# A hybrid decoder layer: products of two weight units in one block, sigmoids behind the last exponentials

## The chip, the cores and the metric

The kernel runs on one core of a Trainium2 chip. The engines that matter are TensorE (PE in the profile; its weight loads are listed as PEld), VectorE (DVE), ScalarE (ACT), GpSimd (POOL) and SyncE (SP, which issues the DMAs). Each works through its own queue in order and waits on semaphores of the others. The metric is the device time of one execution in microseconds; the span in a profile runs from the first to the last instruction, so it is a little shorter.

## The reference, cut to what matters

One decoder layer over 256 positions of width 1024, in float32:

```python
proj  = x @ w_in[l]                      # [q | k | v | B | C | h | gate_attn | gate_conv]
gates = sigmoid(proj[..., off + 3*c:] + b_gate[l])
q, k  = apply_partial_rope(q, cos, sin), apply_partial_rope(k, cos, sin)   # first 16 of 64 dims
y_att = moba_attention(q, k, v) @ w_attn_out[l]
y_cnv = (gate_b * causal_dwconv(gate_c * h_in, conv_w_mix[l])) @ w_conv_out[l]
mix   = (g_att * y_att + g_cnv * y_cnv) @ w_o[l]
x     = layer_norm(DEEPNORM_ALPHA * x + mix, ln1_g[l], ln1_b[l])
u     = causal_dwconv(x @ w_up[l], conv_w_ffn[l])
f     = (silu(u[..., :D_FF]) * u[..., D_FF:]) @ w_down[l]
x     = layer_norm(DEEPNORM_ALPHA * x + f, ln2_g[l], ln2_b[l])
```

There are 8 heads of 64, D_FF is 2816, and the MoBA block is 256 positions, so with 256 positions the attention is plain causal attention: scores, masked softmax, probabilities times v.

## The kernel before, in words

**High and low parts.** Every float32 operand of a product is split into a high part (a rounded copy, made by ACT) and a low part (the rest, a subtraction on DVE). A product of two operands is then three products: high x high, high x low, low x high.

**Units.** The weights lie in memory as chunks of 128 x 2048 numbers, in the order of use; a chunk holds two units of 128 x 1024 in most stages. SP loads chunks into three buffers `raw`. `split_h` (L188) issues the DMA of the chunk two further on and lets ACT write the unit's high part `wh`; `split_l` (L194) lets DVE write the low part `wl`. There are nine buffers of each. The splits run `LA` = 4 to 6 units ahead of the products.

**A unit of columns.** `unit_cols_wide` (L328) computes 128 output columns of the transposed result for all 256 positions. Its activations lie as high and low side by side, so one *wide* product of the weight's high part with 512 columns (L334) does two of the three products; eight of them, over eight slices of the inner dimension, are followed by eight *narrow* ones of the weight's low part with the 256 high columns (L336). The result stands in two halves of one PSUM bank of 512 columns, which are added when the bank is emptied: ACT copies the right half into SBUF and DVE adds the left half.

**The stages.** First 34 warm-up products of zeros (L236), while the first data arrive. Then q, k and v for all heads, chunk by chunk (L539-574), 24 wide products of each inner slice. Then the mixer stage: 28 units of columns, two each for h, c and b of the first half of the convolution channels, the same for the second half, and 16 gate units `g0` to `g15`. The first of them is called `C0` in the code. Then the `y` stage: output products of convolution and attention, times the gates (`mix`, L679); then `w_o` with the first layer norm; then the feed-forward stage and the second layer norm.

**The order in the mixer stage** is written out by hand. `at(u, part, f, ...)` (L463) puts a piece of work beside unit `u`, and `slot(u, products)` (L468) issues, in this order: the unit's products; the PE pieces and then the ACT pieces beside this unit, each in the order in which `at` was called; the split of the high part for unit `u+5`; the split of the low part for unit `u+4`; the DVE pieces, again in the order of the calls. Since engines work in order, this order decides who stands behind whom. Beside the units run:

- `rope` on q and k at C0 and C0+1 (DVE); their transposes on PE, two groups at C0+2 and two at C0+3, and the splits of these one unit later (`qk_h` on ACT, `qk_l` on DVE);
- for head pairs p = 0 to 3: `scores` at C0+4+3p (PE), `masked` one later (DVE), `exps` two later (ACT, exponential); `normalize` at C0+7+5p (DVE), `probs_T` one later (PE, six transposes), `probs_h` and `probs_l` two and three later, `attend` four later (PE), `attend_h` and `attend_l` five later;
- the convolution (`conv1` to `conv4`) and, for every unit, the sum of the two halves of its bank one unit later (`conv_sum_*`, `gate_sum_*`);
- `gate(j)`, the sigmoid of gate unit j on ACT, one unit after its sum. `exps` and `gate` need different function tables of ACT; a change of table is an instruction of its own, ACT_TABLE_LOAD.

Four PSUM banks `acc` serve the units in turn, four banks `ps` serve transposes, scores and attention. The sums of the gates have three buffers `gs`.

**The feed-forward stage** goes over 22 blocks of 128 gate columns (`g`) and 128 value columns (`v`); block i is computed as unit `g`, unit `v`, and the down projection `d` of block i-3, which is 12 wide products (L877). The first two blocks come from another form of product (`up0`) and are transposed by `up0_T`, which is issued behind the first `g` unit of block 2. Both units of a block share a tile of two banks, of which there are two, and the tile is emptied behind unit `v` (`ffn0_act`, `ffn0_dve`). The `slot` of this stage (L916) is a separate function that also runs the splits ahead.

Of the kernel before, what the change touches and what calls it, by code (L numbers as in the profile page):

```python
# [12 lines left out]
AF = mybir.ActivationFunctionType  # L13
ALU = mybir.AluOpType

P = 128
S = 256
# [120 lines left out]
def layer_kernel(ctx: ExitStack, tc: tile.TileContext, x, wpack, cpack, ln1_g, ln1_b, ln2_g, ln2_b, out):  # L138
    nc = tc.nc
# [10 lines left out]
    def acc_bank(name):  # L150
        return psum.tile([P, 512], F32, tag="acc", name=name)

    def ps_bank(name):
        return ps_pool.tile([P, 512], F32, tag="ps", name=name)

    def scratch(shape, name, bufs=None, tag="scr"):
        return tmp.tile(shape, F32, tag=tag, name=name, bufs=bufs or 6)
# [5 lines left out]
    chunks, plan_units, U = plan()  # L163
    blocks = transfers(chunks, plan_units)
    units = [dict(chunk=c, off=off, shape=(k, n), h=None, l=None) for c, off, k, n, _ in plan_units]
# [22 lines left out]
    def split_h(u):  # L188

        issue_dma(units[u]["chunk"] + RAW_BUFS - 1)  # L190
        alloc(u, "h", "wh")
        nc.scalar.activation(units[u]["h"], raw_of(u), AF.Copy)  # L192

    def split_l(u):  # L194

        alloc(u, "l", "wl")
        nc.vector.tensor_tensor(units[u]["l"], raw_of(u), units[u]["h"].bitcast(F32), op=ALU.subtract)  # L197
# [34 lines left out]
    def warm_up(n):  # L232
        for i in range(n):
            nc.tensor.matmul(warm[:, 0:P], zeros, zeros, start=True, stop=True)

    warm_up(34)  # L236

    mask = cst.tile([P, 384], F32, name="mask")
    nc.gpsimd.memset(mask, 0.0)
# [19 lines left out]
    xT = big.tile([P, KT, 2, S], F32R, tag="xT", name="xT")  # L259
# [5 lines left out]
    def bias_gate(j):  # L265
        return consts[:, 132 + j:133 + j]
# [51 lines left out]
    def unit_cols(u, o, bh, bl, n0=0):  # L318

        un = units[u]  # L320
        nk = un["shape"][0]
        for k in range(nk):
            wh, wl = un["h"][:, k, n0:n0 + P], un["l"][:, k, n0:n0 + P]
            nc.tensor.matmul(o, wh, bh[:, k, :], start=k == 0, stop=False)  # L324
            nc.tensor.matmul(o, wh, bl[:, k, :], start=False, stop=False)  # L325
            nc.tensor.matmul(o, wl, bh[:, k, :], start=False, stop=k == nk - 1)  # L326

    def unit_cols_wide(u, bank, b):  # L328


        un = units[u]
        nk = un["h"].shape[1]
        for k in range(nk):
            nc.tensor.matmul(bank, un["h"][:, k, :], b[:, k].rearrange("p a s -> p (a s)"), start=k == 0, stop=False)  # L334
        for k in range(nk):
            nc.tensor.matmul(bank[:, 0:S], un["l"][:, k, :], b[:, k, 0], start=False, stop=k == nk - 1)  # L336

    LA = 4
    cur = {"u": 0}

    def ahead(u):
        for v in range(cur["u"], u + LA + 1):
            split(v)
        cur["u"] = max(cur["u"], u + LA + 1)
# [118 lines left out]
    def at(u, part, f, *a):  # L463
        beside.setdefault(u, {}).setdefault(part, []).append((f, a))
# [3 lines left out]
    def slot(u, products=None):  # L468


        if products:
            products()
        mine = beside.pop(u, {})
        for f, a in mine.get("pe", []) + mine.get("act", []):
            f(*a)
        while done["h"] <= u + LA + 1:
            if units[done["h"]]["h"] is None:
                split_h(done["h"])
            done["h"] += 1
        while done["l"] <= u + LA:  # L480
            if units[done["l"]]["l"] is None:
                split_l(done["l"])
            done["l"] += 1
        for f, a in mine.get("dve", []):
            f(*a)
# [9 lines left out]
    C0 = U[(OFF_H, 0)]  # L495
    for t in range(2):
        at(C0 + t, "dve", rope, t)
    for i, g2 in enumerate((0, 2, 1, 3)):
        at(C0 + 2 + i // 2, "pe", qk_transpose, g2)
        at(C0 + 3 + i // 2, "act", qk_h, g2)  # L500
        at(C0 + 3 + i // 2, "dve", qk_l, g2)
    for p in range(4):
        s = C0 + 4 + 3 * p
        at(s, "pe", scores, p)
        at(s + 1, "dve", masked, p)
        at(s + 2, "act", exps, p)
        s = C0 + 7 + 5 * p
        at(s, "dve", normalize, p)
        at(s + 1, "pe", probs_T, p)
        for j in range(2):  # L510
            at(s + 2 + j, "act", probs_h, p, j)
            at(s + 2 + j, "dve", probs_l, p, j)
        at(s + 4, "pe", attend, p)
        at(s + 5, "act", attend_h, p)
        at(s + 5, "dve", attend_l, p)
# [21 lines left out]
    banks = [[acc_bank(f"{m}{t}") for t in range(2)] for m in "qk"] + [[ps_bank(f"v{t}") for t in range(2)]]  # L537
# [40 lines left out]
    CB = {}  # L578

    def conv_sum_act(nm, pr, e):  # L580

        if e == 0:
            CB["s", nm, pr] = scratch([P, 2, S], f"c{nm}{pr}")
        nc.scalar.activation(CB["s", nm, pr][:, e], CB[nm, pr, e][:, S:2 * S], AF.Copy)

    def conv_sum_dve(nm, pr, e):
        s = CB["s", nm, pr][:, e]
        nc.vector.tensor_tensor(s, CB[nm, pr, e][:, 0:S], s, op=ALU.add)

    def conv1(pr):  # L590
        z = scratch([P, 2, S + 2], f"z{pr}", tag="z", bufs=1)
# [26 lines left out]
    for pr, (c1, c2, c3, c4) in enumerate(((6, 10, 11, 13), (13, 16, 18, 21))):  # L618
        at(C0 + c1, "dve", conv1, pr)
        at(C0 + c2, "act", conv2_act, pr)  # L620
        at(C0 + c2, "dve", conv2_dve, pr)
        at(C0 + c3, "dve", conv3, pr)
        at(C0 + c4, "act", conv4_act, pr)
        at(C0 + c4, "dve", conv4_dve, pr)
        for nm, off in (("h", OFF_H), ("c", OFF_C), ("b", OFF_B)):
            for e in range(2):
                at(U[(off, pr)] + e + 1, "act", conv_sum_act, nm, pr, e)
                at(U[(off, pr)] + e + 1, "dve", conv_sum_dve, nm, pr, e)


    GB = {}
# [10 lines left out]
    def gate(j):  # L642
        nc.scalar.activation(gates[:, j % 8, j // 8, :], GB.pop(("s", j)), AF.Sigmoid, bias=bias_gate(j))

    for j in range(16):
        u = U[("g", 0)] + j
        at(u + 1, "act", gate_sum_act, j)
        at(u + 1, "dve", gate_sum_dve, j)
        if j < 15:
            at(u + 2, "act", gate, j)  # L650


    def unit_bank(u, name):
        bank = acc_bank(name)
        slot(u, lambda: unit_cols_wide(u, bank, xT))
        return bank

    for pr in range(2):
        for nm, off in (("h", OFF_H), ("c", OFF_C), ("b", OFF_B)):
            for e in range(2):  # L660
                CB[nm, pr, e] = unit_bank(U[(off, pr)] + e, f"{nm}{pr}{e}")
    for j in range(16):
        if j == 2:
            gates = big.tile([P, 8, 2, S], F32, tag="b16", name="gates")
        GB[j] = unit_bank(U[("g", 0)] + j, f"g{j}")

    slot(U[("g", 0)] + 16)
    cur["u"] = done["l"]


# [14 lines left out]
    def mix_hl(i):  # L685
        hl_split(mT[:, 0, i, :], mT[:, 1, i, :], M.pop(i))

    for half in range(2):
        for e in range(2):
            ua, uc = U[("ao", half)] + e, U[("co", half)] + e  # L690
            for n in range(2):
                i = half * 4 + e * 2 + n
                if i > 1:
                    mix_hl(i - 2)
                ahead(uc + n - 1)
                bank = ps_bank(f"y{i}")
                unit_cols(uc, bank[:, 256:512], yT[:, 0], yT[:, 1], n * P)
                unit_cols(ua, bank[:, 0:256], aT[:, 0], aT[:, 1], n * P)
                if i == 0:
                    gate(15)  # L700
                mix(i, bank)


# [18 lines left out]
    x1T = big.tile([P, KT, 2, S], F32R, tag="xT", name="x1T")  # L722
# [26 lines left out]
    banks = [acc_bank(f"o0{nh}") for nh in range(2)]  # L749
# [11 lines left out]
    banks = [acc_bank(f"o1{nh}") for nh in range(2)]  # L761
# [104 lines left out]
    def ps_pair(name):  # L866
        return pairs.tile([P, 2, 512], F32, tag="pair", name=name)
# [37 lines left out]
    for c in range(1, NP // 2):  # L905
        for e in range(2):
            i = 2 * c + e
# [23 lines left out]
    tail_from = next(k for k, s in enumerate(seq) if s[0] == "t")  # L931
    for k, (kind, i, u) in enumerate(seq[:tail_from]):
        if kind == "g":
            pair = ps_pair(f"pb{i}")
            unit_cols_wide(u, pair[:, 0], x1T)
        elif kind == "v":
            unit_cols_wide(u, pair[:, 1], x1T)
            PB[i] = pair
        else:
            down(i)  # L940
        if k == 0:
            up0_T(0)
            up0_T(1)
            pending.extend([(st, p) for p in range(2) for st in (1, 2, 3)])
        stages = take(2 if k > 11 or len(pending) > 6 else 1)
        if kind == "v":
            stages.insert(0, (0, i))
            pending.extend([(st, i) for st in (1, 2, 3)])
        slot(k, stages)
# [81 lines left out]
```

## Time and profile before

| | |
|---|---|
| Median of three runs | 370.42 us |
| Profiled execution | 369.92 us |
| Its span | 368.0 us, 5343 instructions |
| TensorE busy | 358.7 us, 2026 products |
| VectorE busy | 295.4 us |
| ScalarE busy | 220.2 us |
| Bytes moved by DMA | 69.63 MB |

Busy time of an engine is the union of its instructions; a product on PE overlaps the one before it, so a busy PE is not PE at its peak, and the distance between the starts of two products is what counts. In the view of the chain that ended last, each line has start, length, engine, tile and source line, and the length of a piece is its share of the chain, so a row with x8 gives what eight products took in a row. In the timeline a row gives start, length from the first start to the last end, engine, line, operation, output and inputs, and in brackets how long the engine had been idle and who ended that.

### The profile page before, as it was taken

To read this page: it belongs to the slowest core of one execution; us is meant where nothing else is said; L and a number is where in the kernel's file an instruction comes from. 1 tells how busy PE (TensorE), PEld (TensorE's weight loads), DVE (VectorE), ACT (ScalarE), POOL (GpSimd) and SP (SyncE) were. 2 spreads that over 40 slices of the span, in tenths; PEclk is the share of its full clock that TensorE was granted. 3 is DMA by queue.
4 is the path that set the end of the run, shared out by engine and by line. 5 is a ranking of instruction groups with operands and counts; after the bars stand their busy time and mean duration, and the time that the engine had idled before them with its cause. 6 is when DMAs were issued, how large, how long until landed. Compare 5 with 4: busy or idle time off the path is not lost.

```text
span 368.0 us, 5343 instructions
## 1 busy us (share of the span) xinstructions
PE 358.7 (97%) x2026; PEld 312.8 (85%) x2026; DVE 295.4 (80%) x510; ACT 220.2 (60%) x374; POOL 6.9 (2%) x26
## 2 busy tenths in 40 slices
PE   8999999999999999999999999999999999999991
PEld 8888888888888899988888888888888888888891
DVE  5795988697797678869759898988879697899784
ACT  4675767669887564634266676675657467576300
POOL 2000000000000000102000000000000000000000
PEclk9999999999999999999999999999999999999997
DMA  8989555435565544596350836348182635562011
GB/s 281 342 299 342 160 192 198 139 116 155 200 224 200 193 172 131 189 364 217 129 226 4 340 117 229 145 199 311 45 331 89 255 132 223 217 237 108 0 59 57
DMA packets 11241, 69.63 MB, mean 189 GB/s; under 512 B 1232, under 2 KB 1616, under 8 KB 4176
## 3 DMA queue, kind: packets, MB, share of 16 engines
q1 hardware_dynamic: 10496, 67.00, 49.4%
q0 software_dynamic: 576, 2.10, 1.8%
q8 instruction: 16, 0.26, 0.3%
q10 hardware_dynamic: 144, 0.20, 0.1%
q14 instruction: 9, 0.07, 0.1%
HBM read 68.24 MB, written 1.05 MB: 188 GB/s over the span
## 4 chain that ended last, share of the span: by engine, by line
PE 97%; DVE 2%; issue 0%; DVEq 0%
PE pb L334 20%; PE pb L336 10%; PE g L334 8%; PE d L305 5%; PE d L306 5%; PE d L307 5%; PE g L336 4%; PE q L543 3%; PE k L543 3%; PE v L543 3%; PE b L334 2%; PE y L326 2%; PE y L325 2%; PE y L324 2%; PE c L334 2%; PE h L334 2%
## 5 line engine op out<-in xcount | busy, mean ns | idle before, releaser
L197 DVE TENSOR_TENSOR wl<-raw,wh 128x1024 fp32r<-128x1024 f32 x88 | 107.4, 1221 | 23.9 <-ACT wh L192 22.9
L192 ACT ACTIVATE wh<-raw 128x1024 fp32r<-128x1024 f32 x88 | 92.5, 1054 | 24.6 <-DMA raw<-in_wpack 24.6
L334 PE MATMUL pb<-x1T,wh 128*128 128x512 f32 x320 | 79.8, 391 | 0.0
L334 PEld LDWEIGHTS pb<-x1T,wh 128*128 128x128 f32 x320 | 58.5, 188 | 11.1
L220 DVE TENSOR_TENSOR wl<-raw,wh 128x1024 fp32r<-128x1024 f32 (+1 forms) x40 | 40.5, 1046 | 8.3 <-ACT wh L219 8.1
L336 PEld LDWEIGHTS pb<-x1T,wl 128*128 128x128 f32 x320 | 43.6, 190 | 3.1
L336 PE MATMUL pb<-x1T,wl 128*128 128x256 f32 x320 | 44.6, 282 | 0.0
L219 ACT ACTIVATE wh<-raw 128x1024 fp32r<-128x1024 f32 (+1 forms) x40 | 34.9, 910 | 13.3 <-DMA raw<-in_wpack 7.6
L334 PE MATMUL g<-xT,wh 128*128 128x512 f32 x128 | 32.3, 394 | 0.0
L305 PE MATMUL d<-wh,f 128*128 128x512 f32 x80 | 31.3, 391 | 0.0
L306 PE MATMUL d<-wl,f 128*128 128x512 f32 x80 | 31.3, 391 | 0.0
L307 PE MATMUL d<-wh,f 128*128 128x512 f32 x80 | 31.1, 389 | 0.0
L334 PEld LDWEIGHTS g<-xT,wh 128*128 128x128 f32 x128 | 23.0, 188 | 4.2
L794 ACT ACTIVATE fb<-pb 128x512 f32<-128x512 f32 x20 | 11.9, 594 | 19.2 <-PE pb L336 19.1
L812 DVE SCALAR_TENSOR_TENSOR fc<-fb,consts,fc 128x254 f32<-128x254 f32 x40 | 19.3, 483 | 1.4
L810 DVE SCALAR_TENSOR_TENSOR fc<-fb,consts,fc 128x255 f32<-128x255 f32 x40 | 19.1, 477 | 0.0
L336 PEld LDWEIGHTS g<-xT,wl 128*128 128x128 f32 x128 | 17.4, 190 | 1.3
L804 ACT ACTIVATE fc<-fb,consts 128x256 f32<-128x256 f32 x40 | 18.0, 497 | 0.4 <-DVE fb L798 0.4
L336 PE MATMUL g<-xT,wl 128*128 128x256 f32 x128 | 17.8, 282 | 0.0
L307 PEld LDWEIGHTS d<-wh,f 128*128 128x128 f32 x80 | 15.0, 188 | 3.2
L305 PEld LDWEIGHTS d<-wh,f 128*128 128x128 f32 x80 | 15.1, 188 | 2.7
L306 PEld LDWEIGHTS d<-wl,f 128*128 128x128 f32 x80 | 15.1, 188 | 2.6
(183 smaller groups left out, 611.8 us busy)
## 6 DMA issues: line engine op xcount, KB each, us to landing
raw<-in_wpack SPq DMA_DIRECT2D x55, 1024.0 KB, 4.9
raw<-in_wpack SPq DMA_DIRECT2D x6, 896.0 KB, 5.8
xr<-in_x SPq DMA_DIRECT2D x1, 1024.0 KB, 7.1
ln<-in_ln_g POOLq DMA_DIRECT2D x2, 512.0 KB, 5.2
ln<-in_ln_b POOLq DMA_DIRECT2D x2, 512.0 KB, 5.9
raw<-in_wpack SPq DMA_DIRECT2D x3, 256.0 KB, 3.2
raw<-in_wpack SPq DMA_DIRECT2D x1, 512.0 KB, 5.2
out<-x SPq DMA_DIRECT2D x2, 256.0 KB, 2.8
```

The source lines that it names most:

```text
L192: nc.scalar.activation(units[u]["h"], raw_of(u), AF.Copy)
L197: nc.vector.tensor_tensor(units[u]["l"], raw_of(u), units[u]["h"].bitcast(F32), op=ALU.subtract)
L219: nc.scalar.activation(h, src, AF.Copy)
L220: (eng or nc.vector).tensor_tensor(l, src, h.bitcast(F32), op=ALU.subtract)
L305: nc.tensor.matmul(o, ah, bh, start=start, stop=False)
L306: nc.tensor.matmul(o, ah, bl, start=False, stop=False)
L307: nc.tensor.matmul(o, al, bh, start=False, stop=stop)
L334: nc.tensor.matmul(bank, un["h"][:, k, :], b[:, k].rearrange("p a s -> p (a s)"), start=k == 0, stop=False)
L336: nc.tensor.matmul(bank[:, 0:S], un["l"][:, k, :], b[:, k, 0], start=False, stop=k == nk - 1)
L543: nc.tensor.matmul(banks[m][t], (xl if p == 2 else xh)[:, k, t * P:(t + 1) * P], wl if p == 1 else wh, start=k == 0 and p == 0, stop=k == ...
L810: nc.vector.scalar_tensor_tensor(c[:, 1:S], pb[:, a * S:a * S + S - 1], w_ffn(1, j), c[:, 1:S], op0=ALU.mult, op1=ALU.add)
L812: nc.vector.scalar_tensor_tensor(c[:, 2:S], pb[:, a * S:a * S + S - 2], w_ffn(0, j), c[:, 2:S], op0=ALU.mult, op1=ALU.add)
```

## The change

Four things are changed.

1. *Units in twos.* In the mixer and the feed-forward stage, two units are computed as one block: the eight wide products of the first, the eight wide ones of the second, then the narrow ones of the first and those of the second. PE work that stands beside the first unit of a pair is issued between the two wide groups. A bank is complete only at the end of its pair, so all sums of halves in the mixer stage move one unit later.
2. *Sigmoids.* `gate(j)` moves from two units behind gate unit j to three, and not before C0+17, which lies behind the last `exps` at C0+15. The gates 0, 1 and 2 are therefore issued together in slot C0+17. `gate(15)` now falls into the first slot of the `y` stage, and for that a slot is run there.
3. *q's and k's transposes* all go beside C0+2, and their splits beside C0+3. `normalize` is registered ahead of the other attention pieces, so in its slot it precedes `attend_l` on DVE.
4. 30 warm-up products instead of 34.

```diff
-    warm_up(34)
+    warm_up(30)
...
-    def unit_cols_wide(u, bank, b):
+    def cols_wide(u, bank, b):
         un = units[u]
-        nk = un["h"].shape[1]
-        for k in range(nk):
+        for k in range(un["h"].shape[1]):
             nc.tensor.matmul(bank, un["h"][:, k, :], b[:, k].rearrange("p a s -> p (a s)"), start=k == 0, stop=False)
+
+    def cols_narrow(u, bank, b):
+        un = units[u]
+        nk = un["l"].shape[1]
         for k in range(nk):
             nc.tensor.matmul(bank[:, 0:S], un["l"][:, k, :], b[:, k, 0], start=False, stop=k == nk - 1)
+
+    def cols_pair(u, second, banks, b):
+        cols_wide(u, banks[-1], b)
+        if second:
+            cols_narrow(u - 1, banks[0], b)
+            cols_narrow(u, banks[1], b)
...
-    for i, g2 in enumerate((0, 2, 1, 3)):
-        at(C0 + 2 + i // 2, "pe", qk_transpose, g2)
-        at(C0 + 3 + i // 2, "act", qk_h, g2)
-        at(C0 + 3 + i // 2, "dve", qk_l, g2)
+    for g2 in (0, 2, 1, 3):
+        at(C0 + 2, "pe", qk_transpose, g2)
+        at(C0 + 3, "act", qk_h, g2)
+        at(C0 + 3, "dve", qk_l, g2)
+    for p in range(4):
+        at(C0 + 7 + 5 * p, "dve", normalize, p)
...
-        at(s, "dve", normalize, p)
...
-                at(U[(off, pr)] + e + 1, "act", conv_sum_act, nm, pr, e)
-                at(U[(off, pr)] + e + 1, "dve", conv_sum_dve, nm, pr, e)
+                at(U[(off, pr)] + e + 2, "act", conv_sum_act, nm, pr, e)
+                at(U[(off, pr)] + e + 2, "dve", conv_sum_dve, nm, pr, e)
...
-        at(u + 1, "act", gate_sum_act, j)
-        at(u + 1, "dve", gate_sum_dve, j)
-        if j < 15:
-            at(u + 2, "act", gate, j)
+        at(max(u + 3, C0 + 17), "act", gate, j)
+        at(u + 2, "act", gate_sum_act, j)
+        at(u + 2, "dve", gate_sum_dve, j)
...
-    def unit_bank(u, name):
-        bank = acc_bank(name)
-        slot(u, lambda: unit_cols_wide(u, bank, xT))
-        return bank
+    def two_units(u, names):
+        banks = []
+        for e in range(2):
+            banks.append(acc_bank(names[e]))
+            slot(u + e, lambda: cols_pair(u + e, e == 1, banks, xT))
+        return banks
...
-    slot(U[("g", 0)] + 16)
+    for e in range(2):
+        slot(U[("g", 0)] + 16 + e)
...
                 if i == 0:
-                    gate(15)
+                    slot(uc + n)
...
         if kind == "g":
-            pair = ps_pair(f"pb{i}")
-            unit_cols_wide(u, pair[:, 0], x1T)
+            pair, first_unit = ps_pair(f"pb{i}"), u
+            cols_wide(u, pair[:, 0], x1T)
         elif kind == "v":
-            unit_cols_wide(u, pair[:, 1], x1T)
+            cols_wide(u, pair[:, 1], x1T)
+            cols_narrow(first_unit, pair[:, 0], x1T)
+            cols_narrow(u, pair[:, 1], x1T)
```

The loops that call `two_units` go over the units in steps of two; `CB` and `GB` hold the banks by pair.

More of the change, by code (lines that the diff above doesn't have):

```diff
@@ L583, in conv_sum_act @@
             CB["s", nm, pr] = scratch([P, 2, S], f"c{nm}{pr}")
-        nc.scalar.activation(CB["s", nm, pr][:, e], CB[nm, pr, e][:, S:2 * S], AF.Copy)
+        nc.scalar.activation(CB["s", nm, pr][:, e], CB[nm, pr][e][:, S:2 * S], AF.Copy)
     def conv_sum_dve(nm, pr, e):
         s = CB["s", nm, pr][:, e]
-        nc.vector.tensor_tensor(s, CB[nm, pr, e][:, 0:S], s, op=ALU.add)
+        nc.vector.tensor_tensor(s, CB[nm, pr][e][:, 0:S], s, op=ALU.add)
     def conv1(pr):
@@ L646, in layer_kernel @@
         u = U[("g", 0)] + j
-        at(u + 1, "act", gate_sum_act, j)
-        at(u + 1, "dve", gate_sum_dve, j)
-        if j < 15:
-            at(u + 2, "act", gate, j)
-    def unit_bank(u, name):
-        bank = acc_bank(name)
-        slot(u, lambda: unit_cols_wide(u, bank, xT))
-        return bank
+        at(max(u + 3, C0 + 17), "act", gate, j)
[7 more added lines that the diff above has]
+        return banks
     for pr in range(2):
         for nm, off in (("h", OFF_H), ("c", OFF_C), ("b", OFF_B)):
-            for e in range(2):
-                CB[nm, pr, e] = unit_bank(U[(off, pr)] + e, f"{nm}{pr}{e}")
-    for j in range(16):
+            CB[nm, pr] = two_units(U[(off, pr)], [f"{nm}{pr}{e}" for e in range(2)])
+    for j in range(0, 16, 2):
         if j == 2:
             gates = big.tile([P, 8, 2, S], F32, tag="b16", name="gates")
-        GB[j] = unit_bank(U[("g", 0)] + j, f"g{j}")
-    slot(U[("g", 0)] + 16)
+        GB[j], GB[j + 1] = two_units(U[("g", 0)] + j, [f"g{j + e}" for e in range(2)])
+    for e in range(2):
+        slot(U[("g", 0)] + 16 + e)
     cur["u"] = done["l"]
```

## The prediction

> **What bounds the kernel now.** I read the page from the top: busy shares first, then the chain that ended last, then single stretches.
>
> ```profile
> PE 358.7 (97%) x2026; PEld 312.8 (85%) x2026; DVE 295.4 (80%) x510; ACT 220.2 (60%) x374; POOL 6.9 (2%) x26
> ...
> PE 97%; DVE 2%; issue 0%; DVEq 0%
> ...
> 37.90:129.70 91.80, 91.23 (x561) 79.97 (x560) 73.24 (x158) 66.96 (x134) 0.00 (x0) 1.00 0.51 182
> ```
>
> TensorE is busy for 97% of the span and carries 97% of the chain. The last row is the mixer stage (units `h` to `g`, from the windows view; columns are length, then busy time of PE, weight loads, DVE, ACT, POOL): PE lacks 0.57 us of 91.80 there. So an edit is worth only what it takes from the distance between PE instructions, or from one of the few stops of PE. DVE (73.24 of 91.80) and ACT (66.96) count where they make PE wait.
>
> **1. Products in twos.** The chain in order of time (start, length, engine, tile, line) shows what the order of products costs. It credits each piece with the time until the next one.
>
> ```profile
> 210.55 1.81 PE pb L334 x8
> 212.36 0.95 PE pb L336 x8
> 213.31 1.84 PE pb L334 x8
> ...
> 216.11 0.23 PE d L305
> ...
> 129.91 0.12 PE y L324
> ...
> 131.47 0.12 PE y L325
> ```
>
> Eight wide products take 1.81 us behind other wide ones (the `d` group ends at 210.55), but 1.84 behind narrow ones: unit `g` lasts 213.31-210.55 = 2.76, unit `v` 216.11-213.31 = 2.80. Over the same stretch eight narrow products take 0.95, while in a long run of them each takes 0.12 (13 steps in the `y` stage from 129.91 to 131.47), so 0.96 for eight. A pair now changes from narrow to wide twice and will do so once: about 0.03 less, and the second eight narrow products lose the 0.01 that the first of a run gains. I take 0.02 us a pair; the rounding of the rows bounds it at 0 and 0.04.
>
> This holds for pairs with nothing between their units. There are 34 pairs: 14 in the mixer, 20 in the feed-forward stage. In eight, other PE work is issued after the first unit and will now stand between two wide groups: the transposes of q and k, `scores` 0 and 2, `probs_T` 0 and 2, `attend` 1 and 3, and `up0_T`. What a transpose costs there, against behind narrow products:
>
> ```profile
> 46.39 0.87 PE qkt L372 x8
> 47.27 1.84 PE c L334 x8
> ...
> 54.61 2.05 PE b L334 x8
> ...
> 172.02 0.87 PE x1t L773 x8
> 172.90 0.23 PE o L305
> ...
> 174.74 0.23 PE o L307
> ```
>
> Behind narrow products eight transposes take 0.87 and the next eight wide ones 1.84; behind wide ones (`x1t`) it is 0.87 and 174.74-172.90 = 1.84 again. So these pairs save nothing and lose the 0.01. `scores` behind a wide group does not occur; behind narrow ones the next wide group takes 2.05, 0.21 over 1.84, so each of the two could win or lose up to 0.2; I take 0. Sum: 26 x 0.02 - 8 x 0.01 = **0.44 us less** (bounds: 0.5 more, 1.4 less, from the rounding and `scores`).
>
> The first narrow group now comes 1.8 us later and the second wide one 0.95 earlier. Both operands are split four units (about 11 us) ahead, so the splits cover this.
>
> The Trainium skill (TensorE: Matmul & The Clock Gate, Back-to-back issue gap) prices a product alone by its own columns, N/2.4 + 2.5 ns, whatever stands before it: 109 ns narrow, 216 ns wide. By that rule this edit would bring 0. The trace has 120 and 227 ns, and a price on the change of kind, so I follow the rows.
>
> **2. The one stop of PE in the mixer.**
>
> ```profile
> 97.80 0.42 DVE gs L640
> ...
> 102.02 1.85 PE g L334 x8
> ...
> 114.24 1.84 PE g L334 x8
> ...
> 117.69 1.39 PE g L334 x6
> ```
> ```profile
> 101.15 0.33 PE L429 MATMUL ptp<-ident,sm 128*128 128x128 f32 x1 [0.57 <-DVE sm L423]
> ```
>
> In the mixer the chain leaves PE only here, at 97.80 for DVE: `probs_T(2)` waits for `normalize(2)` (second fence, the timeline of PE). One unit with its transposes lasts 117.69-114.24 = 3.45 undisturbed and 102.02-97.80 = 4.22 here (the unit starts at 97.80 too), so the stop costs **0.77 us**. Why DVE was late:
>
> ```profile
> 88.60 1.28 ACT L413 ACT_TABLE_LOAD   x1
> ...
> 91.78 1.28 ACT L643 ACT_TABLE_LOAD   x1
> ...
> 93.88 0.42 DVE L640 TENSOR_TENSOR gs<-g,gs 128x256 f32<-128x256 f32 x1 [3.94 <-ACT gs L636]
> ...
> 99.27 0.85 DVE L216 TENSOR_TENSOR aT<-av,aT 64x256 fp32r<-64x256 f32 x2
> 100.13 0.18 DVE L419 RECIPROCAL st<-st 128x4 f32<-128x4 f32 x1
> 100.35 1.01 DVE L423 TENSOR_SCALAR sm<-sm,st 128x128 f32<-128x128 f32 x4
> ```
>
> ACT went from the sigmoid to the exponential and back (two table loads) and DVE stood 3.94 us for the gate sum behind them. Then `attend_l(1)` ran before `normalize(2)`. The change takes both loads away (2.56 us of ACT) and puts `normalize` first (0.85). `normalize(2)` ended at 100.35+1.01 = 101.36; it should now end near 101.36-2.56-0.85 = 97.95. `probs_T(2)` is issued behind the wide group alone, 0.95 before 100.41 (= 97.80+1.84+0.95, less rounding, of the undisturbed unit), so at about 99.6. Cover: 1.6 us. The new order alone would give 100.51, too late; the loads alone would do. I take the whole 0.77 (bounds 0 and 0.77).
>
> **3. What comes late next.** Every accumulator bank is now emptied only when its pair is done, one slot later, and four banks are two pairs. The tightest I find is the bank of `g3`, needed by `g7` at 99.6 + 0.65 (six transposes) = 100.2. In that slot ACT's queue holds the two `attend_h(1)` copies, then a table load and gates 0, 1 and 2 in a row, and only behind them the copy of `g3` and the split of a later weight.
>
> ```profile
> 93.95 0.23 PE av L305
> ...
> 97.11 0.76 ACT L452 ACTIVATE aT<-av 64x256 fp32r<-64x256 f32 x2
> ...
> L643 ACT ACTIVATE gates<-gs,consts 128x256 f32<-128x256 f32 x16 | 8.1, 507 | 2.9 <-DVE gs L640 2.8
> ```
>
> `attend(1)` will start 0.95 earlier (93.0) and takes 1.05 (93.95 to the unit at 95.00 that follows), the copies end near 94.9, the load and three sigmoids take 1.28 + 3 x 0.51 = 2.8, so 97.7; copy 0.37 and DVE sum 0.42 give 98.5. Cover 1.7 us: nothing added.
>
> q's and k's transposes all come behind the wide group of the third unit. They need `rope(1)`:
>
> ```profile
> 44.30 0.28 DVE L364 TENSOR_TENSOR qk<-ra,rb 128x128 f32<-128x128 f32 x1
> ```
>
> It ends at 44.58; the first transpose would go at 46.39-0.95 = 45.4. Cover 0.8. The eight splits behind them (four ACT, four DVE) have until `scores(0)`, two units on. The DMA issues ride on the splits' order, which is unchanged up to the end of the gates; there one further unit is split ahead, on ACT and DVE, while PE has 23 us of `y` products that wait for neither. Cost 0. In the feed-forward stage banks are emptied after the second unit, as before: 0.
>
> **4. Four warm-ups fewer.**
>
> ```profile
> 0.99 3.81 PE L234 MATMUL warm<-zeros 128*128 128x128 bf16 x34 [0.99 <-DVE zeros L224]
> ...
> 3.66 0.43 DVE L552 CAST wh<-raw 128x512 fp32r<-128x512 f32 x1
> ...
> 4.56 0.78 PE L543 MATMUL q<-wh,xT 128*128 128x512 f32 x1
> 5.13 0.63 PE L543 MATMUL q<-wh,xT 128*128 128x512 f32 x1
> 5.56 0.49 PE L543 MATMUL q<-wh,xT 128*128 128x512 f32 x1
> 5.89 0.39 PE L543 MATMUL q<-wh,xT 128*128 128x512 f32 x1
> 6.12 0.63 PE L543 MATMUL q<-wl,xT 128*128 128x512 f32 x2
> ```
>
> A warm-up takes (4.56-0.99)/34 = 0.105; four are 0.42. The weight for the first real product is there at 4.09, and without them PE would be free at 4.14. But the first products run at about half speed (5.13 to 5.56: 0.43, against 0.23 later), up to about 5.8, though the page's clock row shows full speed. So the 0.42 us won hold one slow product instead of two: **0.20 us less** (bounds 0 and 0.42). The next chunk is the nearest operand that could then be late:
>
> ```profile
> 7.98 0.69 DVE L220 TENSOR_TENSOR wl<-raw,wh 128x512 fp32r<-128x512 f32 x1
> ...
> 9.48 1.36 PE q L543 x6
> ```
>
> Its low half is there at 8.67, 0.8 before the chain shows its group, more than the 0.42 won.
>
> The Trainium skill (the same page, Part 1: The HAM clock gate) says that PE runs at half rate until a free-running window of 3.4 us has been busy, so the turn moves between runs. The trace agrees with half rate (0.43 a product); its turn lies 4.8 us after the first warm-up. By that rule the number of warm-ups does not set the turn.
>
> **The sum:** 0.44 + 0.77 + 0.20 = 1.41 us. The profiled execution took 369.92 us, 1.9 of it outside the span of 368.0: it becomes 368.5 (span 366.6). The median of the runs shown is 370.42, 0.5 above it, so I forecast **369.0 us** as the median, own range 368.2 to 369.7.
>
> **The rivals.**
> *Grouping saves nothing* (0.15): the rows show 0.03 between two groups, near their rounding, and sixteen narrow products in a row might build up a debt that the next wide group pays in full. Against it: behind the `y`-like narrow runs each product stays at 0.12. 370.42-0.97 = 369.5.
> *The late bank, slower than before* (0.08): the block of load and sigmoids on ACT holds back the copy of `g3`; if DVE's hole of 3.94 us stays as long, the sum comes at 98.5+3.94 = 102.4 and PE stands 2.2 us at `g7`. -0.64 + (2.2-0.77) = +0.8: 371.2. It decides once ACT is 1.7 us later than worked out, and makes the kernel slower from 3.1 us. Against it: both table loads that made the hole are gone.
> *The speed turns later* (0.07): if PE is idle for a moment behind 30 warm-ups and its 4.8 us count anew from the first product, the turn falls at 4.14+4.8 = 8.9 instead of 5.8. At 0.43 against 0.23 a product, 3.1 us more at half speed cost 1.4: 370.4. Against it: the weight is there 0.05 us before PE is free. The window of the Trainium skill (the same section) would make it 3.4 us more and, as an estimate, 1.6.
> *The wait stays* (0.05): `probs_T(2)` finds `normalize` late by as much as before: 369.8.
>
> **How the numbers follow.** My forecast has 0.60, the four rivals 0.35, anything else 0.05. The range reaches over the rivals to 371.2, and below to 367.8 for all gains at their upper bounds (370.42-1.4-0.77-0.42). A change under 2% (7.4 us) cannot be told from none in this kernel; no case reaches it, so within 2% has 0.96, slower 0.03 for a stop that I missed in every pair, faster 0.01.
>
> **What would show it.** Right: wide groups of 1.81 behind wide ones in `pb` and `g`, triples `g v d` 0.02 shorter, no stop before `ptp`, two table loads fewer, the first `q` product near 4.14. Wrong: a stop of PE ahead of a wide `g` group with the releaser DVE `gs`, or half-speed products after 6 us.

## The result

| | before | after |
|---|---|---|
| Median of six runs | 370.42 us | 368.99 us |
| Profiled execution, span | 369.92, 368.0 us | 369.0, 367.1 us |
| Products of PE | 2026 | 2022 |
| Table loads on ACT | 7 | 5 |

The ratio of after to before is 0.9958, with an interval of [0.9944, 0.9972]: 1.0 to 2.1 us less. The forecast was 369.0. One of the six runs before took 602.16 us and is not in the ratio. The ratios here and below are taken over the runs and are not the quotients of the two medians beside them (here 0.9961). The prediction says that a change under 2% cannot be told from none; this interval tells 0.4% from none.

The page after, and a row of its windows view that holds the mixer stage, over the same stretch as before (length, then busy time of PE, weight loads, DVE, ACT, POOL):

```profile
PE 358.0 (98%) x2022; PEld 312.2 (85%) x2022; DVE 294.9 (80%) x510; ACT 217.0 (59%) x372; POOL 7.0 (2%) x26
...
37.90:129.70 91.80, 91.80 (x567) 80.42 (x566) 74.22 (x159) 64.85 (x134) 0.00 (x0) 1.00 0.52 184
```

PE no longer lacks anything of that stretch (91.80 of 91.80; before, 91.23), and ACT is 2.1 us less busy there.

Four rows of the chain in order of time cut a kernel into stages: the first product of the mixer (`h`), the first of the `y` stage, the first of the feed-forward stage (`pb`), and the last product of all (`e`). Before:

```profile
38.04 1.81 PE h L334 x8
...
129.91 0.12 PE y L324
...
187.47 1.81 PE pb L334 x8
...
360.11 0.13 PE e L307
```

After:

```profile
38.42 3.63 PE h L333 x16
...
129.44 0.12 PE y L324
...
187.00 1.82 PE pb L333 x8
...
359.27 0.13 PE e L307
```

The differences are the stages. The mixer went from 91.87 to 91.02 (0.85 less), the feed-forward stage from 172.64 to 172.27 (0.37 less), what lies between (`y`, `w_o` and the first blocks of the feed-forward stage) stayed at 57.56. What lies ahead of the mixer went up, from 38.04 to 38.42 in these two executions. So the steady part of the gain is 1.22 us, inside the interval, and the start needs runs of its own.

The stop is gone. In the chain after, `probs_T(2)` (line 440) follows its wide group at once:

```profile
98.13 1.84 PE g L333 x8
99.97 0.11 PE ptp L440
...
100.63 1.85 PE g L333 x8
```

### The profile page after: what moved, and what is told of

It reads as the page before. It is cut to its first block, busy times and chain, and to the rows that moved or that the text cites. A ratio compares the mean times of both kernels' runs of the same rounds, so it can differ in the third digit from the quotient of the medians.

```text
span 367.1 us, 5335 instructions
## 1 busy us (share of the span) xinstructions
PE 358.0 (98%) x2022; PEld 312.2 (85%) x2022; DVE 294.9 (80%) x510; ACT 217.0 (59%) x372; POOL 7.0 (2%) x26
## 4 chain that ended last, share of the span: by engine, by line
PE 97%; DVE 1%; DMA 1%; DVEq 0%; SPq 0%; issue 0%
PE pb L333 20%; PE pb L340 10%; PE g L333 8%; PE d L305 5%; PE d L306 5%; PE d L307 5%; PE g L340 4%; PE q L555 3%; PE k L555 3%; PE v L555 3%; PE b L333 2%; PE y L326 2%; PE y L325 2%; PE y L324 2%; PE c L333 2%; PE o L307 2%
## 5 line engine op out<-in xcount | busy, mean ns | idle before, releaser
L197 DVE TENSOR_TENSOR wl<-raw,wh 128x1024 fp32r<-128x1024 f32 x90 | 109.8, 1221 | 23.3 <-ACT wh L192 22.7
L192 ACT ACTIVATE wh<-raw 128x1024 fp32r<-128x1024 f32 x90 | 94.5, 1055 | 22.7 <-DMA raw<-in_wpack 22.6
L333 PE MATMUL pb<-x1T,wh 128*128 128x512 f32 x320 | 76.2, 390 | 0.0
L333 PEld LDWEIGHTS pb<-x1T,wh 128*128 128x128 f32 x320 | 59.7, 188 | 12.1
L220 DVE TENSOR_TENSOR wl<-raw,wh 128x1024 fp32r<-128x1024 f32 (+1 forms) x38 | 38.0, 1037 | 7.4 <-ACT wh L219 7.1
L340 PEld LDWEIGHTS pb<-x1T,wl 128*128 128x128 f32 x320 | 41.0, 191 | 1.6
L340 PE MATMUL pb<-x1T,wl 128*128 128x256 f32 x320 | 41.5, 283 | 0.0
L219 ACT ACTIVATE wh<-raw 128x1024 fp32r<-128x1024 f32 (+1 forms) x38 | 32.9, 904 | 14.3 <-DMA raw<-in_wpack 8.5
L340 PEld LDWEIGHTS g<-xT,wl 128*128 128x128 f32 x128 | 16.4, 191 | 0.6
L340 PE MATMUL g<-xT,wl 128*128 128x256 f32 x128 | 16.6, 283 | 0.0
```

What stands on the lines that cost most here:

```text
L219: nc.scalar.activation(h, src, AF.Copy)
L220: (eng or nc.vector).tensor_tensor(l, src, h.bitcast(F32), op=ALU.subtract)
```

## The experiments

**The feed-forward stage alone.** The kernel before, with its feed-forward blocks in twos (`cols_wide` and `cols_narrow` as in the change; this cut and the following ones show the lines that matter):

```diff
-            unit_cols_wide(u, pair[:, 0], x1T)
+            first_unit = u
+            cols_wide(u, pair[:, 0], x1T)
         elif kind == "v":
-            unit_cols_wide(u, pair[:, 1], x1T)
+            cols_wide(u, pair[:, 1], x1T)
+            cols_narrow(first_unit, pair[:, 0], x1T)
+            cols_narrow(u, pair[:, 1], x1T)
```

> The kernel before, with the products in twos in the feed-forward stage alone. If a change from narrow to wide products costs what the rows show (0.03 us, less 0.01 for the second narrow group), 19 plain pairs save 0.02 each: 0.4 us, ratio 0.9990, and a triple g v d lasts 8.28 us instead of 8.30. If sixteen narrow products in a row build up a debt that the next wide group pays, a triple stays at 8.30 and the ratio is 1.000. The mixer's stop of 0.77 us stays in both.

Measured: 369.65 against 370.01 us, ratio 0.9986 [0.9976, 0.9997]. Its chain (stage limits, and one block with the next):

```profile
187.58 1.82 PE pb L341 x8
...
359.85 0.13 PE e L307
```

```profile
202.34 3.63 PE pb L341 x16
205.96 1.91 PE pb L347 x16
...
210.62 3.63 PE pb L341 x16
```

The stage lasts 359.85-187.58 = 172.27, as in the changed kernel, 0.37 less than before, while its mixer stage stays at 91.86. Sixteen wide products take 3.63 = 2 x 1.81, so the second group no longer pays the 0.03. A triple (`g`, `v`, `d`) lasts 210.62-202.34 = 8.28, as expected; before it was 218.85-210.55 = 8.30. The differences are small but they repeat: the stage takes 172.26 to 172.28 in all seven profiles with pairs in it, and 172.64 or 172.65 in all four without. Grouping does save, and no debt follows.

**The stop alone.** The kernel before, one unit at a time and with 34 warm-ups, with the sigmoids and `normalize` moved, and with them the sums of the gates, one unit later:

```diff
+    for p in range(4):
+        at(C0 + 7 + 5 * p, "dve", normalize, p)
...
-        at(s, "dve", normalize, p)
...
-        at(u + 1, "act", gate_sum_act, j)
-        at(u + 1, "dve", gate_sum_dve, j)
-        if j < 15:
-            at(u + 2, "act", gate, j)
+        at(max(u + 3, C0 + 17), "act", gate, j)
+        at(u + 2, "act", gate_sum_act, j)
+        at(u + 2, "dve", gate_sum_dve, j)
...
```

> The kernel before, with its units one by one and 34 warm-ups, but the sigmoids behind the last exponentials, the gates' sums one slot later and normalize ahead of attend_l. If the two table loads and the place of normalize make the stop before probs_T(2), it is gone: 0.77 us less, ratio 0.9979, no idle time before ptp and two table loads fewer. If the stop came from DVE's load as such, or the block of three sigmoids makes a new one, the time stays within 0.3 us of before.

Measured: 369.40 against 370.01 us, ratio 0.9986 [0.9974, 0.9997]. The mixer stage in its chain:

```profile
37.97 1.81 PE h L334 x8
...
129.04 0.12 PE y L324
```

It lasts 91.07, 0.80 less than before. So of the 0.85 in the mixer the stop is 0.80, and 0.05 is left for the grouping and the moved transposes of q and k, which no run takes apart.

**The order alone.** The kernel before, with `normalize` ahead of `attend_l` and nothing else; the loads stay:

```diff
+    for p in range(4):
+        at(C0 + 7 + 5 * p, "dve", normalize, p)
...
-        at(s, "dve", normalize, p)
```

> The kernel before with normalize ahead of attend_l and nothing else: the loads stay, units one by one. By the prediction's sum normalize(2) ends 0.85 us earlier, at 100.51 against 100.41 wanted: the stop shrinks from 0.8 to 0.1 us, mixer stage 91.2 instead of 91.87. If the table loads alone made the stop, it stays near 0.8 and the stage at 91.9.

Measured: 369.37 against 370.36 us, ratio 0.9980 [0.9966, 0.9994]. Its chain:

```profile
38.35 1.81 PE h L334 x8
...
129.42 0.12 PE y L324
```

and the timelines of DVE, `normalize(2)`, and of PE, the first transpose behind it:

```profile
99.80 1.01 DVE L423 TENSOR_SCALAR sm<-sm,st 128x128 f32<-128x128 f32 x4
```

```profile
100.73 0.27 PE L429 MATMUL ptp<-ident,sm 128*128 128x128 f32 x1
```

The stage lasts 91.07, as in the experiment on the stop: the order alone removes the whole stop of the kernel before. `normalize(2)` ends at 100.81 and its first transpose starts at 100.73, with no idle time before it, so it just fits. The expectation had 0.1 us of stop left, because it set the end of `normalize(2)` (100.51) against the first transpose (100.41). But the transposes start before that end: here 0.08 us before it, and in the kernel before, where PE waited for it, 0.21 (101.15 against 101.36).

**The loads alone.** The changed kernel, with `normalize` again behind `attend_l`:

```diff
-    for p in range(4):
-        at(C0 + 7 + 5 * p, "dve", normalize, p)
...
+        at(s, "dve", normalize, p)
         at(s + 1, "pe", probs_T, p)
```

> The changed kernel, but normalize again behind attend_l on DVE; the sigmoids stay behind the last exponentials. By the prediction the table loads alone were enough (normalize(2) at 98.8, wanted at 99.6): no stop, mixer stage 91.0 us, same time as the changed kernel. If the order counts, PE stops before probs_T(2) for 0.1 us or more.

Measured: 368.95 against 369.96 us, ratio 0.9965 [0.9953, 0.9977]. Chain, and `normalize(2)` on DVE:

```profile
37.74 3.63 PE h L333 x16
...
128.76 0.12 PE y L324
```

```profile
96.40 1.01 DVE L434 TENSOR_SCALAR sm<-sm,st 128x128 f32<-128x128 f32 x4
```

The stage lasts 91.02, as with the new order. Without the two loads the order is not needed in the changed kernel.

**The loads back, first try.** The changed kernel without the limit at C0+17:

```diff
-        at(max(u + 3, C0 + 17), "act", gate, j)
+        at(u + 3, "act", gate, j)
```

> The changed kernel, but the sigmoids only three units behind their gate unit and not behind the last exponentials, so the two table loads come back; normalize stays ahead of attend_l. By the prediction the order alone is not enough: normalize(2) ends near 100.5 on its scale and probs_T(2) would go at 99.6, so PE stops for about 0.9 us there and the mixer stage lasts 91.9 us instead of 91.0. If the order was what removed the stop, the stage stays at 91.0 and the loads cost nothing.

Measured: 368.33 against 369.96 us, ratio 0.9952 [0.9939, 0.9966], mixer stage 91.03. But the loads did not come back: five, as in the changed kernel, since gate 0 falls into the slot of the last exponentials and stands behind them there. The run does not test the order. It shows that the later sums alone already put the sigmoids behind the exponentials, and that the limit at C0+17 brings nothing to the mixer stage (91.03 without it, 91.02 with it).

**The loads back, second try.** Gate 0 is put ahead of the last exponentials in their slot:

```diff
-        at(max(u + 3, C0 + 17), "act", gate, j)
+        at(u + 3, "act", gate, j)
+        if j == 0:
+            at(C0 + 15, "act", exps, 3)
...
-        at(s + 2, "act", exps, p)
+        if p < 3:
+            at(s + 2, "act", exps, p)
```

> The changed kernel, with the sigmoid of gate 0 ahead of the last exponentials in slot C0+15 and the other sigmoids three units behind their gate unit, so that the two table loads are really there again (six or seven loads, not five); normalize stays ahead of attend_l. (Without a gate ahead of the last exponentials the loads did not come back.) By the prediction's sum (cover 1.6 us with both, 2.56 of it from the loads) PE stops before probs_T(2) for about 0.9 us: mixer stage 91.9 us. By the changed kernel's own trace (normalize ends at 97.2, the transposes go at 99.8: cover 2.6) the two loads just fit: stop below 0.2 us, stage 91.0 to 91.2.

Measured: 370.88 against 370.36 us, ratio 1.0018 [1.0003, 1.0032], seven loads. The mixer stage lasts from 39.02 to 132.23 = 93.2 us:

```profile
39.02 3.63 PE h L333 x16
...
132.23 0.12 PE y L324
```

The timelines of ACT, DVE and PE in that stretch:

```profile
89.42 1.28 ACT L656 ACT_TABLE_LOAD   x1 [2.09 <-DVE gs L653]
```

```profile
94.70 0.42 DVE L653 TENSOR_TENSOR gs<-g,gs 128x256 f32<-128x256 f32 x1 [3.77 <-ACT gs L649]
```

```profile
95.18 2.14 PE L333 MATMUL g<-xT,wh 128*128 128x512 f32 x8 [0.20 <-DVE gs L653]
...
101.64 0.33 PE L440 MATMUL ptp<-ident,sm 128*128 128x128 f32 x1 [0.44 <-DVE sm L434]
...
103.22 2.09 PE L333 MATMUL g<-xT,wh 128*128 128x512 f32 x8 [0.70 <-DVE gs L653]
```

DVE's hole is back at 3.77 us, and PE stops three times: before the transposes, and twice before a wide group, for a bank that DVE's gate sum has not emptied (at 95.18 `g5`, at 103.22 `g7`). The idle times, 0.20, 0.44 and 0.70, count from the modelled end of a product, so the stage loses more than their sum: it is 2.2 us longer than in the changed kernel. That is more than either expectation had. ACT here also waited 2.09 us for the sum of gate 0, which stands ahead of the exponentials, so the price is not that of the loads alone, and the run does not tell how much of it is theirs. Every engine does the same work in both kernels but for two loads of 1.28 us on ACT, which is busy for 60% of the span.

**Wide and narrow by turns.** The changed kernel, with every narrow product right behind its wide one in the feed-forward stage:

```diff
+    def cols_mixed(u, bank, b):
+        un = units[u]
+        nk = un["h"].shape[1]
+        for k in range(nk):
+            nc.tensor.matmul(bank, un["h"][:, k, :], b[:, k].rearrange("p a s -> p (a s)"), start=k == 0, stop=False)
+            nc.tensor.matmul(bank[:, 0:S], un["l"][:, k, :], b[:, k, 0], start=False, stop=k == nk - 1)
...
```

> The changed kernel, but in the feed-forward stage each wide product is followed at once by its narrow one, unit by unit. If every change from narrow to wide products has a price of 0.027 us, a unit lasts 8 x (0.227+0.113+0.027) = 2.94 us instead of 2.78 and the 40 units cost 6.4 us more (about 375.4). If the price is a debt that a run of narrow products builds up, because a weight is ready only every 0.12 us while a narrow product takes 0.113, then each wide product of 0.227 pays for its neighbour and a unit lasts 8 x 0.34 = 2.72 us: 2.4 us less (about 366.6).

Measured: 370.32 against 369.96 us, ratio 1.0007 [0.9998, 1.0016]; the feed-forward stage lasts 360.89-186.85 = 174.04, 1.77 more than in the changed kernel. The limits of the stage in its chain, then one block, its first product and the first of the `d` group behind:

```profile
186.85 0.23 PE pb L346
...
360.89 0.13 PE e L307
```

```profile
201.60 0.23 PE pb L346
...
207.24 0.23 PE d L305
```

A block (units `g` and `v`) takes 5.64 us here, 5.54 in the changed kernel, 5.56 in the kernel before. Neither theory holds: the first had 5.88 for two units, the second 5.44. Fifteen changes from narrow to wide inside the block cost 0.10 together, where one costs 0.03 in the kernel before, so a change has no fixed price; and a wide product does not pay for its narrow neighbour either. Long runs are the best of the three orders.

**The warm-ups.** The kernel before with 30, the changed kernel with 34 and with 16:

```diff
-    warm_up(34)
+    warm_up(30)
```

> The kernel before with 30 warm-ups instead of 34 and nothing else. Forecast of the prediction: 0.20 us less, ratio 0.9995, first q product near 4.14 us. Rival, the landing: the first q product starts when its weight has come by DMA, and the warm-ups only fill the time; then it starts at the landing plus about 0.9 us wherever that is later than 4.14, and the time changes by 0 to 0.2 us, less than the spread of the runs. Rival, the speed: fewer warm-ups let PE turn to full speed later, about 0.2 us or more lost; then the turn lies later than 4.8 to 5.3 us after the first warm-up.

```diff
-    warm_up(30)
+    warm_up(34)
```

> The changed kernel with 34 warm-ups again. By the prediction's step it is 0.20 us slower than the changed kernel (369.2). By the landing it is equal within 0.1 us (369.0). By the speed it is faster (368.8 or less). In its profile the first q product starts at the later of 4.56 us and the landing of the weight plus 0.9 us.

```diff
-    warm_up(30)
+    warm_up(16)
```

> The changed kernel with 16 warm-ups: PE is idle from about 2.7 us until the first weight has landed (first q product at 4.2 to 4.8). If the turn to full speed needs PE to stay busy until then, the turn comes later than the 4.4 to 6.5 us seen so far and the mixer stage starts later than 38.4 us (time up by 0.3 us or more). If the turn goes by time alone or by the landing, the stage starts at 37.8 to 38.4 as with 30 and 34 and the time is the same.

Measured: before with 30, 370.03 against 370.01 us, ratio 0.9999 [0.9990, 1.0009]; changed with 34, 368.75, ratio 0.9964 [0.9950, 0.9977]; changed with 16, 370.24 against 369.96, ratio 1.0002 [0.9992, 1.0012]. In the changed kernel the start looks like this (timeline of DVE, then of PE):

```profile
4.30 0.43 DVE L564 CAST wh<-raw 128x512 fp32r<-128x512 f32 x1 [0.68 <-DMA raw<-in_wpack]
```

```profile
0.99 3.38 PE L234 MATMUL warm<-zeros 128*128 128x128 bf16 x30 [0.99 <-DVE zeros L224]
4.78 1.86 PE L555 MATMUL q<-wh,xT 128*128 128x512 f32 x4 [0.41 <-DVE wh L564]
6.48 0.63 PE L555 MATMUL q<-wl,xT 128*128 128x512 f32 x2
```

The first weight landed later here than in the kernel before (its cast starts at 4.30, there at 3.66), PE waited 0.41 us for it, and the first four products took until 6.48. In the kernel before with 30 warm-ups, and in the loads-alone run (also 30):

```profile
4.24 2.07 PE L543 MATMUL q<-wh,xT 128*128 128x512 f32 x4
6.11 0.87 PE L543 MATMUL q<-wl,xT 128*128 128x512 f32 x2
```

```profile
4.80 1.20 PE L554 MATMUL q<-wh,xT 128*128 128x512 f32 x4 [0.43 <-DVE wh L563]
```

The one starts at 4.24 and its first four products run at half speed; the other starts at 4.80, is at full speed almost at once (1.20 for four overlapping products against 2.07), and reaches the mixer at 37.74, earlier than any kernel with 34. An early turn is not enough, though. In two other profiles with 30 warm-ups the first four products also took only 1.19, but PE then waited for the weights that follow (by turns; loads back, second try):

```profile
9.68 0.50 PE L562 MATMUL q<-wl,xT 128*128 128x512 f32 x1 [0.23 <-DVE wl L220]
```

```profile
8.14 0.74 PE L556 MATMUL v<-wh,xT 128*128 128x512 f32 x2 [0.62 <-ACT wh L219]
```

Their mixers start at 38.31 and 39.02. So between 30 and 34 neither the end of the warm-ups nor their number sets the start. It goes by the landing of the first data, by the moment at which PE turns to full speed, and by the weights behind the first, and all three move from one execution to the next. (One inner slice of q, k and v is 18 products, x6 each in the chain, not 24.) Over the profiles the mixer starts at 38.04, 38.16, 37.97, 38.54 and 38.35 with 34 warm-ups and at 38.42, 38.28, 37.83, 37.74, 38.31 and 39.02 with 30.

With 16, PE stands idle before the first product:

```profile
4.75 2.08 PE L555 MATMUL q<-wh,xT 128*128 128x512 f32 x4 [1.87 <-DVE wh L564]
6.62 1.05 PE L555 MATMUL q<-wl,xT 128*128 128x512 f32 x2
7.47 0.80 PE L555 MATMUL k<-wh,xT 128*128 128x512 f32 x2
```

The first product comes when it came with 30 (4.75 and 4.78), but half speed lasts until about 7.9 and the mixer starts at 39.14, 0.7 later than in the profile of the changed kernel and later than in any profile with 30 or 34. The stages behind are unchanged (91.02, 57.56 and 172.27), so it is the start that uses up the gain of the change (ratio 1.0002, not 0.9958). Sixteen warm-ups, which leave PE idle for 1.87 us before the data, are too few here; between 30 and 34 no difference shows beyond the spread of the runs.

## Why the prediction was right, step by step

**1. Products in twos: right in mechanism and size.** 0.44 us were forecast, 0.02 for each of 26 plain pairs less 0.01 for eight others. Measured: 0.37 in the feed-forward stage (forecast 19 x 0.02 - 0.01 = 0.37) and 0.05 in the mixer (forecast 7 x 0.02 - 7 x 0.01 = 0.07). The chain after, one block and the next:

```profile
201.76 3.63 PE pb L333 x16
205.38 1.91 PE pb L340 x16
207.30 0.23 PE d L305
...
210.04 3.63 PE pb L333 x16
```

Sixteen narrow products take 1.91, just the 0.01 more than 2 x 0.95. The rival that grouping saves nothing is out. The formula by columns alone that the Trainium skill gives (TensorE: Matmul & The Clock Gate, Back-to-back issue gap) has no term for the order of products, and here the order counts; the section gives it for an isolated product and says that in a stream the loads of weights set the spacing too. But the picture behind the step, a price on each change, is wrong: by turns a change costs less than 0.01 us (0.10 for fifteen). What the cost hangs on stays open.

**2. The stop: right, 0.77 forecast and 0.80 measured.** But of the two causes named, one is enough: the order alone removes the stop in the kernel before, and taking the loads away alone is enough in the changed kernel. (The loads alone were not taken out of the kernel before.) The step had `normalize(2)` at 100.51 with the order alone, and too late. On the scale of that run's mixer start (38.35 against 38.04) it ended at 100.50, as forecast, and that was in time for the kernel before. The step's 100.41 for the first transpose there is not the sum that it gives, 97.80+1.84+0.95 = 100.59; it agrees with the timeline, where the narrow group ahead starts at 99.46 and takes 0.95 (the chain shows the starts of PE some 0.2 later). "Too late" can hold only for the changed kernel, where the transposes come 0.95 earlier. That was not tried apart from ACT's other wait in the last loads run.

**3. What comes late next: right, and the covers were close.** After, on DVE and ACT:

```profile
95.20 1.28 ACT L655 ACT_TABLE_LOAD   x1
96.50 1.31 ACT L655 ACTIVATE gates<-gs,consts 128x256 f32<-128x256 f32 x3
```

```profile
90.60 0.42 DVE L652 TENSOR_TENSOR gs<-g,gs 128x256 f32<-128x256 f32 x1 [0.28 <-ACT gs L648]
...
96.20 1.01 DVE L434 TENSOR_SCALAR sm<-sm,st 128x128 f32<-128x128 f32 x4
...
98.25 0.42 DVE L652 TENSOR_TENSOR gs<-g,gs 128x256 f32<-128x256 f32 x1 [0.28 <-ACT gs L648]
```

The sum of `g3` ended at 98.67, and the wide group of `g7` starts at 100.63 in the chain; less the 0.38 by which this mixer starts later, 98.3 and 100.25, where the step had 98.5 and 100.2. `normalize(2)` ended at 97.21, 96.8 on the same scale, a microsecond ahead of the step's 97.95, because DVE's hole shrank from 3.94 us to 0.28 (the row at 90.60), by 3.66 and not just by the 2.56 of the loads. The late bank did not come here. The last loads run shows it at the place that the rival had: with DVE's hole back, PE stops at `g7`, and the kernel is slower than before. But the sizes agree only by chance: the rival had 2.2 us at `g7` alone, while the run loses 2.2 us at three places, of which `g7` is one (0.70 us idle).

**4. Four warm-ups fewer: wrong.** The step had 0.20 us less. The runs show 0.0 (ratio 0.9999 [0.9990, 1.0009] for the edit alone), and in the profiled executions the mixer starts 0.38 later. The step that failed took one profile's landing (the weight at 4.09) and one turn (about 5.8) as fixed; over the profiles with 30 or 34 the first product starts between 4.24 and 4.80 and the mixer between 37.74 and 39.02. Two of the prediction's own signs came out against this step: the first product came at 4.78, not near 4.14, and half-speed products lasted until 6.48. Its cover of 0.8 us for the weight of the next chunk is not safe either: PE waited for its low half in the run by turns (0.23 us) and in that of the order alone (0.22). The Trainium skill (TensorE: Matmul & The Clock Gate, Part 1: The HAM clock gate) says that the turn moves between runs. The runs agree in that: the first four products took 1.17 to 2.07 us with 30 or 34 warm-ups. The rival that the speed turns later shows only once PE is idle for long (1.87 us with 16 warm-ups); an idle time of 0.41 to 0.43 before the first product went with a late turn in one profile and an early one in another.

Without the term of the warm-ups the sum is 1.21, and the steady stages give 1.22; the forecast would then have been 369.2. That the median fell on 369.0 within 0.01 us is luck beyond that: the runs of the changed kernel spread over 1 us (368.26 to 369.28).

## What to carry to other kernels

Where PE carries the chain, cut the kernel into stages by its first products and compare the stages: the same stage of the same code repeats to 0.04 us or better here (91.02, 91.02, 91.03, 91.02 and 90.98 for the mixer in pairs), while whole times spread over 1 us, and a change of 0.4% can be split into its parts that way. Two functions of ACT from different tables that take turns cost 1.28 us a table load here, and the harm came from the engine behind them: DVE stood for 3.94 us. In the kernel before another order on DVE was enough to hide that; in the changed kernel, where buffers are released later, much the same hole (3.77 us) went with stops of PE at three places. A cover read from one execution is good for work that hangs on PE, and not for work that hangs on the first DMA.

## What was not expected of the hardware

PE's turn to full speed moves by 1.7 us or more between executions. In one (loads back, first try) the first product starts at 4.39 us and is almost at full speed at once, 1.19 us for four; in another (the kernel before with 30) products are still at half speed after 6.1. Both had 30 warm-ups, and the clock row of the profile shows full speed all the while. The 0.38 us by which the mixer started later in the profile of the changed kernel is within the spread of the starts (37.74 to 39.02).

A product of 512 columns behind one of 256 costs up to 0.03 us more than behind its like, and not in proportion to the number of changes: eight wide and eight narrow products take 2.76 to 2.80 us in runs and 2.82 by turns (5.64 for two units).
